# One gate group of the token-major projection moved behind the z groups, in a hybrid GatedDeltaNet and retention block

## The chip, the core and the metric

The kernel runs on one core of a Trainium2 chip. The core has five engines with an instruction queue each: TensorE (PE, matmuls, with its weight loads listed apart), VectorE (DVE), ScalarE (ACT), GpSimd (POOL) and SyncE (SP), which here only issues DMA transfers. Each engine runs its instructions in the order of the program made for it and waits on semaphores for the others. The metric is the device time of one execution in microseconds.

## The reference, cut to what matters

One layer of a diffusion backbone works on 1024 latent and 256 context tokens, D = 1024, all in float32. All projections come from one matrix, w_in; four heads of 128 are gated DeltaNet, four are retention.

```
p = (h @ w_in).astype(f32)                 # h: 256 context + 1024 latent tokens
qkv_a, z, ab, rq, rk, rv, rg = jnp.split(p, splits, axis=-1)
qkv_a = short_conv(...)                    # 5 taps, then silu
q, k, v = ...                              # q, k normalized
# gated delta rule, forward and backward, per chunk of 64:
A   = strict lower part of (beta k k^T) * decay
sol = triangular_solve(A + I, [beta v, beta k exp(G)])
# scan over the chunks with the solved rows
o_gdn = rms_norm(o_f + o_b) * silu(z)
o_ret = head_group_norm(r_f + r_b) * silu(rg)      # retention, rotary q and k
x = x + g1 * (concat(o_gdn, o_ret) @ w_out)
x = x + g2 * swiglu(...)
```

The columns `rg` (512 of them, the gate of the retention heads) are computed and passed through silu long before they are used: they multiply the retention's output at the end of the mixer. `z` is the same for the delta rule's output.

## The kernel before

Every float32 matmul is split into a high and a low half: `whi·hhi`, `wlo·hhi`, `whi·hlo`, three matmuls for one (lines 371 to 373 in `tm_half`, 611 to 613 in `conv_block`). ScalarE rounds the raw weights to `whi`, VectorE (or GpSimd) subtracts for `wlo` (L344, L345).

The projections whose result is wanted with tokens on partitions go by `token_major(g, ...)`. There are ten groups `g` of 256 columns, two for each of rv, rk, rq, rg and z, in this order of numbers: 6 and 7 are the retention's gate, 8 and 9 are z, 2 and 3 rk. A latent group has 8 tiles of 128 tokens and 24 matmuls a tile, 192 matmuls. The bank is called `tm`; gate and z groups leave it through `fin_gate`, a Silu on ScalarE (L532) into `res`, and a store to DRAM. The weights come from a pool with two buffers: `W`, which the convolutions use too, or `W2`, opened for the first groups and closed before the chunk preparation.

The stages around the change, in the order of the code:

1. `conv_block` for k, then q (blocks 4 to 7 and 0 to 3): matmuls into `b2`, two evictions on ScalarE (`u`, `y`: L614, L615), taps on VectorE (L621), Silu (L624).
2. `token_major` of the gate groups 6 and 7, then the pools `R2` and `W2` are closed, and the pools of the chunk preparation (`gu`, `gi`, `gp`) open over their space.
3. Chunk preparation, `pre(t)`, for ten chunks in three batches, `[0,1,2,9]`, `[3,8,4,7]`, `[5,6]`. PE multiplies `kk` (L705), transposes q (`qt`, L710) and multiplies `kq` (L715). For each of two directions SP loads a row of decays to all partitions (`gw`, L718), GpSimd masks it to `e` (L722), ScalarE takes the exp per head (L726) and then of `gw` itself (L735), VectorE multiplies `ut` (L730) and `sp` (L732), GpSimd the second half of `sp` (L736). All of `gw`, `e`, `ut`, `sp` have two buffers.
4. `invert(b)` after each batch: the 32 x 32 diagonal blocks of the triangular matrix are inverted by 31 serial steps, each a product (L765) and a subtraction (L767) on VectorE. Its inputs `L` come from a load `yr`, copied by ScalarE (L758) and VectorE (L759); `X` is cleared by GpSimd (L755).
5. The four v convolution blocks, their transposes `vT` (L856) and evictions `vt` (L859). `vT` and `tm` share three PSUM buffers.
6. `merge(b)`: small matmuls `m` (L807 to L834) join the inverted blocks, from `U` and `t`, loaded back from DRAM (`xd`, `un`).
7. `token_major` of z, groups 8 and 9, in pool `W`.
8. The scan: two directions, ten steps each, from loads `pk`; its first matmuls are `Tr` (L922). The remaining groups, rk among them, are computed beside it. Then come the retention, the output projection and the feed-forward part.

The order of each engine's instructions isn't that of the code. The program is made under a scheduler that simulates a timeline and lets each engine take what its simulation finds ready, so stages 3 to 8 run interleaved, and a change in one place moves rows in others. A buffer that is used again is waited for tile by tile.

Of the kernel before, what the change touches and what calls it, by code (L numbers as in the profile page):

```python
# [38 lines left out]
def build(nc, tc, ap, dbg=None, stop=None, marks=None):  # L39
    root = ExitStack()  # L40
    V, S, G, T, SY = nc.vector, nc.scalar, nc.gpsimd, nc.tensor, nc.sync

    def pool(name, bufs=1, side=None, space=None):
        kw = {}
        if side is not None:
            kw["side"] = side
        if space is not None:
            kw["space"] = space
        if space is not DRAM:
            kw["reuse_waits"] = "tile"  # L50
        es = ExitStack()
        p = es.enter_context(tc.tile_pool(name=name, bufs=bufs, **kw))
        root.push(es)
        p_close[id(p)] = es
        return p
# [10 lines left out]
    def checkpoint(name):  # L66
        if dbg is not None:
            marks.append((name, int(nc.cur_bb.bb.instructions[-1].name.split("-")[-1])))
        if stop == name:
            raise Stop()  # L70
# [120 lines left out]
    try:  # L191
# [40 lines left out]
        W2 = None  # L232
# [127 lines left out]
        def tm_weights(g, kh, pl, q=S):  # L360
            return weights(ap["wt"][g, :, 4 * kh:4 * kh + 4, :], [4, 256], V, pl, q, raws.get((g, kh)), g == 0)

        def tm_bank(g):
            return bank_a("tm")[:, 0:WIDE if g == 0 else 256]

        def tm_half(o, w, kh, t):

            tsl = slice(t * P, (t + 1) * P)
            whi, wlo = w
            for k in range(4 * kh, 4 * kh + 4):  # L370
                T.matmul(o, hhi[:, k, tsl], whi[:, k % 4, :], start=(k == 0), stop=False)  # L371
                T.matmul(o, hhi[:, k, tsl], wlo[:, k % 4, :], start=False, stop=False)  # L372
                T.matmul(o, hlo[:, k, tsl], whi[:, k % 4, :], start=False, stop=(k == KT - 1))  # L373
# [5 lines left out]
        def tm_store(g, t, o, finish, store, pl):  # L379
            early = g < 2  # L380
            res = (W2 if early else R1).tile([P, 256], F32, tag="res", name="res", bufs=4 if early else 2)
            finish(t, o[:, 0:256], res)
            if g == 0:
                S.activation(xa[:, t, :], o[:, 256:WIDE], AF.Copy)
            nm, c0 = GROUPS[g // 2], (g % 2) * 256
            dst = zd[t - 2, :, c0:c0 + 256] if nm == "z" else rd[t, :, RD[nm], c0:c0 + 256]
            store.dma_start(dst, res)

        def token_major(g, tiles, finish, store, pl, q=S):

            w = [tm_weights(g, kh, pl, q) for kh in range(2)]

            for p in range(0, len(tiles), 2):
                pair = [(t, tm_bank(g)) for t in tiles[p:p + 2]]
                for kh in range(2):
                    for t, o in pair:
                        tm_half(o, w[kh], kh, t)
                for t, o in pair:
                    tm_store(g, t, o, finish, store, pl)
# [47 lines left out]
        W2 = pool("w2", bufs=2)  # L447
# [86 lines left out]
        LAT, ALL = list(range(2, TT)), list(range(2, TT)) + [0, 1]  # L534
# [148 lines left out]
                        y[:, NCTX:].rearrange("p (t j) -> p t j", j=P))  # L683

        checkpoint("q")
        for g in (6, 7):
            token_major(g, LAT, fin_gate, S, W2, SY)
        checkpoint("rg")
        close(R2)
        close(W2)  # L690
# [185 lines left out]
        merge(2)  # L876


        for g in (8, 9):
            token_major(g, LAT, fin_gate, S, W)  # L880
        checkpoint("rgz")
        close(GM)
# [772 lines left out]
```

## Time and profile before

| | |
|---|---|
| median of 3 runs | 1476.76 us (1476.37 to 1479.9) |
| profiled execution | 1477.96 us, of which the trace's span 1476.2 us |
| granted TensorE clock, mean | 0.983 |
| PE busy | 1397.2 us, 95% of the span |
| VectorE busy | 964.6 us, 65% |
| ScalarE busy | 614.0 us, 42% |
| GpSimd busy | 590.3 us, 40% |

Times in the trace are microseconds from the start of the span. A row of a list of instructions has start, length, engine, line, operation, output and inputs, shape, and in brackets the idle time before it and what ended that. A row of waits has the engine and its line, what it waited for, then the total, the number of times and the longest. Group rows end in busy time, mean ns of one, and idle time before. Line numbers of the kernel before are used; in the changed kernel all lines behind the first edit are one lower.

The stages above lie here in the trace: the last gate group's matmuls 249 to 276, chunk preparation and v convolutions to 377, z and the merges to 473, the scan from 473, the retention from 580.

### The profile page before, as it was taken

How to read it: one execution, taken by the hardware profiler on the slowest of the kernel's cores; microseconds unless marked ns; L12 is line 12 of the kernel's file. 1: busy time of each engine (PE TensorE's matmuls, PEld its weight loads, DVE VectorE, ACT ScalarE, POOL GpSimd, SP SyncE). 2: the span in 40 equal slices, each digit the busy share in tenths (PEclk: the TensorE clock that was granted, in tenths of full speed). 3: DMA queues.
4: the chain of work that ended last, by engine and by line, in shares of the span. 5: the costliest groups of instructions: out<-in, count | busy, mean ns of one | idle time of the engine just before them, and what ended most of it. 6: DMA issues, size and time to landing. Idle time of an engine off the chain costs nothing.

```text
span 1476.2 us, 24111 instructions
## 1 busy us (share of the span) xinstructions
PE 1397.2 (95%) x8919; PEld 1199.2 (81%) x8919; DVE 964.6 (65%) x1856; ACT 614.0 (42%) x1326; POOL 590.3 (40%) x501
## 2 busy tenths in 40 slices
PE   7999999986789999899799899999999999999997
PEld 2898888975689999898688688877888888788885
DVE  6566789289792435689676877556555564657477
ACT  5643564587333111245443623233333332444445
POOL 0120010243202344234144688898555552335321
PEclk9999999998899999999899999999999999999999
DMA  9536686688888625996532265674222242776863
GB/s 337 197 105 205 189 249 200 219 264 277 282 216 277 238 76 178 416 341 209 184 125 104 97 238 210 242 264 162 105 97 105 107 151 79 260 260 194 288 216 114
DMA packets 170421, 298.14 MB, mean 202 GB/s; under 512 B 43496, under 2 KB 93880, under 8 KB 165952
## 3 DMA queue, kind: packets, MB, share of 16 engines
q1 hardware_dynamic: 118752, 253.17, 50.2%
q10 hardware_dynamic: 49072, 35.83, 7.8%
q0 software_dynamic: 2480, 7.60, 1.4%
q8 instruction: 70, 1.15, 0.3%
q14 instruction: 47, 0.39, 0.1%
HBM read 206.60 MB, written 89.96 MB: 201 GB/s over the span
## 4 chain that ended last, share of the span: by engine, by line
PE 55%; POOL 6%; DMA 5%; DVE 4%; issue 2%; ACT 2%; SPq 1%; ACTq 0%; POOLq 0%; DVEq 0%
PE ffn L1344 7%; PE ffn L1342 6%; PE ffn L1343 6%; PE fo L1470 4%; PE fo L1469 4%; PE fo L1468 4%; PE tm L371 3%; PE tm L373 3%; PE tm L372 3%; PE op L1203 2%; PE op L1201 2%; PE op L1202 2%; DMA wd<-tw 2%; POOL ws L1315 1%; DMA pk<-sd 1%
## 5 line engine op out<-in xcount | busy, mean ns | idle before, releaser
L371 PE MATMUL tm<-whi,hhi 128*128 128x256 f32 (+1 forms) x704 | 199.5, 287 | 7.7 <-ACT vt L859 3.4
L372 PE MATMUL tm<-wlo,hhi 128*128 128x256 f32 (+1 forms) x704 | 199.3, 285 | 2.4 <-issue 2.0
L373 PE MATMUL tm<-whi,hlo 128*128 128x256 f32 (+1 forms) x704 | 197.7, 285 | 0.0
L371 PEld LDWEIGHTS tm<-whi,hhi 128*128 128x128 f32 x704 | 132.8, 190 | 11.8 <-ACT vt L859 3.6
L1342 PE MATMUL ffn<-t,whi 128*128 128x512 f32 x352 | 136.9, 390 | 1.3 <-ACT whi L344 1.3
L1344 PE MATMUL ffn<-t,wlo 128*128 128x512 f32 x352 | 137.0, 390 | 1.0 <-DVE wlo L345 1.0
L1343 PE MATMUL ffn<-t,whi 128*128 128x512 f32 x352 | 137.0, 389 | 0.0
L372 PEld LDWEIGHTS tm<-wlo,hhi 128*128 128x128 f32 x704 | 133.7, 190 | 2.1 <-issue 0.9
L373 PEld LDWEIGHTS tm<-whi,hlo 128*128 128x128 f32 x704 | 132.8, 190 | 2.6 <-issue 1.8
L344 ACT ACTIVATE whi<-wraw 128x512 fp32r<-128x512 f32 (+2 forms) x98 | 75.1, 771 | 141.4 <-PE ffn L1343 80.5
L344 ACT ACTIVATE whi<-ws 128x512 fp32r<-128x512 f32 x88 | 55.6, 632 | 171.5 <-PE ffn L1343 123.4
L345 DVE TENSOR_TENSOR wlo<-ws,whi 128x512 fp32r<-128x512 f32 x88 | 93.9, 1068 | 47.0 <-ACT whi L344 46.8
L1469 PE MATMUL fo<-wlo,ahi 128*128 128x512 f32 x308 | 120.2, 390 | 2.1 <-DVE wlo L345 2.1
L1468 PE MATMUL fo<-whi,ahi 128*128 128x512 f32 x308 | 119.3, 390 | 0.7 <-ACT ahi L344 0.7
L1470 PE MATMUL fo<-whi,alo 128*128 128x512 f32 x308 | 119.0, 390 | 0.0
L345 DVE TENSOR_TENSOR wlo<-wraw,whi 128x512 fp32r<-128x512 f32 (+2 forms) x92 | 99.4, 1082 | 24.6 <-ACT whi L344 24.6
L1342 PE MATMUL ffn<-b,whi 128*128 128x512 f32 x264 | 103.8, 393 | 4.4 <-ACT whi L344 4.4
L1344 PE MATMUL ffn<-b,wlo 128*128 128x512 f32 x264 | 103.6, 393 | 0.8 <-DVE wlo L345 0.8
L1343 PE MATMUL ffn<-b,whi 128*128 128x512 f32 x264 | 103.4, 392 | 0.0
L612 PE MATMUL b<-hlo,whi 128*128 128x512 f32 (+1 forms) x256 | 94.4, 369 | 0.0
L613 PE MATMUL b<-hhi,wlo 128*128 128x512 f32 (+1 forms) x256 | 94.3, 368 | 0.0
L611 PE MATMUL b<-hhi,whi 128*128 128x512 f32 (+1 forms) x256 | 94.3, 368 | 0.0
(446 smaller groups left out, 3448.1 us busy)
## 6 DMA issues: line engine op xcount, KB each, us to landing
adaw<-ada SPq DMA_DIRECT2D x48, 512.0 KB, 4.4
pk<-sd SPq DMA_DIRECT2D x16, 1536.0 KB, 10.0
wraw<-wfi SPq DMA_DIRECT2D x44, 512.0 KB, 3.7
ar<-ad SPq DMA_DIRECT2D x33, 512.0 KB, 4.7
w<-wfo SPq DMA_DIRECT2D x22, 512.0 KB, 5.7
wd<-tw SPq DMA_DIRECT2D x11, 1024.0 KB, 4.8
ad<-act SPq DMA_DIRECT2D x20, 512.0 KB, 3.0
raw<-wd SPq DMA_DIRECT2D x20, 512.0 KB, 4.9
```

The source lines that it names most:

```text
L344: S.activation(hi, raw, AF.Copy)
L345: e.tensor_tensor(lo, raw, hi.bitcast(F32), ALU.subtract)
L371: T.matmul(o, hhi[:, k, tsl], whi[:, k % 4, :], start=(k == 0), stop=False)
L372: T.matmul(o, hhi[:, k, tsl], wlo[:, k % 4, :], start=False, stop=False)
L373: T.matmul(o, hlo[:, k, tsl], whi[:, k % 4, :], start=False, stop=(k == KT - 1))
L612: T.matmul(o, whi[:, k, :], hl, start=False, stop=False)
L1342: T.matmul(o, whi[:, k, :], xhi(xn, slice(0, 4), k), start=(first and k == 0), stop=False, **kw)
L1343: T.matmul(o, whi[:, k, :], xlo(xn, slice(0, 4), k), start=False, stop=False, **kw)
L1344: T.matmul(o, wlo[:, k, :], xhi(xn, slice(0, 4), k), start=False, stop=(k == 3), **kw)
L1468: T.matmul(po[g][i], ahi[:, ts], whi, start=(j == 0 and not kw), stop=False, **kw)
L1469: T.matmul(po[g][i], ahi[:, ts], wlo, start=False, stop=False, **kw)
L1470: T.matmul(po[g][i], alo[:, ts], whi, start=False, stop=(j == FH - 1), **kw)
```

## The change

Group 7, the second half of the retention's gate columns, is no longer computed with group 6 but after the z groups. Its call has the default pool `W` and ScalarE's queue for the weight load, where it had `W2` and SP's queue. So `R2` and `W2` are closed, and the pools of the chunk preparation opened, behind group 6.

```diff
         checkpoint("q")
-        for g in (6, 7):
-            token_major(g, LAT, fin_gate, S, W2, SY)
+        token_major(6, LAT, fin_gate, S, W2, SY)
         checkpoint("rg")
         close(R2)
         close(W2)
@@
-        for g in (8, 9):
+        for g in (8, 9, 7):
             token_major(g, LAT, fin_gate, S, W)
         checkpoint("rgz")
```

The scheduler makes new orders from this. Three places show it.

On PE, after the last matmuls of group 6 (bank `tm_2590`): before, the v convolution (`b2`) is broken off for the tiles of group 7, `tm_2657` to `tm_2826`, whose last rows and the first `kk` behind them are

```order
L372 MATMUL tm_2826<-wlo_2652,hhi_86 128x256
L373 MATMUL tm_2826<-whi_2651,hlo_87 128x256
L705 MATMUL kk_2897<-kc_2895 128x128 x4
L705 MATMUL kk_2930<-kc_2928 128x128 x4
L613 MATMUL b2_3572<-hhi_86,wlo_3539 128x512
```

and now the v convolution's matmuls run on without a tile of group 7, up to

```order
L612 MATMUL b2_3463<-hlo_87,whi_3429 128x512
L613 MATMUL b2_3463<-hhi_86,wlo_3430 128x512
L611 MATMUL b2_3463<-hhi_86,whi_3429 128x512
L704 MATMUL kk_2661<-kc_2659 128x128 x4
L612 MATMUL b2_3463<-hlo_87,whi_3429 128x512
```

The first `kk` stood behind all 192 matmuls of group 7 and 35 of the convolutions; it now stands behind 103 matmuls of the convolutions, in the second block.

On ScalarE, at the exps of the last chunk (`e_4137` and `e_4155` before, `e_3901` and `e_3919` now, one for each direction): before, the last convolution's Silu `y_3918` and all z tiles came behind them,

```order
L726 ACTIVATE e_4137<-e_4137,nG_1284 128x128 x3
L735 ACTIVATE gw_4135<-gw_4135 128x512
L712 ACTIVATE qt_4121,nq_1292<-qt_4121 128x128
L726 ACTIVATE e_4155<-e_4155,nG_1284 128x128 x4
L735 ACTIVATE gw_4153<-gw_4153 128x512
```

and now the Silu of z tiles (`res`, L532) stands between them, with loads of the activation table:

```order
L725 ACTIVATE e_3901<-e_3901,nG_1284 128x128 x4
L734 ACTIVATE gw_3899<-gw_3899 128x512
L532 ACT_TABLE_LOAD
L532 ACTIVATE res_4838<-tm_4788 128x256
L387 DMA zd_116<-res_4838 128x256
L532 ACTIVATE res_4841<-tm_4789 128x256
L387 DMA zd_116<-res_4841 128x256
L757 ACTIVATE L_3196<-yr_3191 64x1024
L725 ACT_TABLE_LOAD
L725 ACTIVATE e_3919<-e_3919,nG_1284 128x128 x4
```

The program has 24 table loads in all, where it had 20. On VectorE the product `ut` of `e_3919` now stands behind the third product of the second inversion; before, it came within the first.

On PE at the scan's first matmuls: before, tiles of the rk group (`tm_5542` to `tm_5674`) stood ahead of them,

```order
L372 MATMUL tm_5675<-wlo_5531,hhi_86 128x256
L373 MATMUL tm_5675<-whi_5530,hlo_87 128x256
L371 MATMUL tm_5674<-whi_5536,hhi_86 128x256
L372 MATMUL tm_5674<-wlo_5537,hhi_86 128x256
L834 MATMUL m2_4917<-U2_4813,xt2_4918 64x64 x16
L922 MATMUL Tr_5444<-pk0_5440 128x128 x4
```

and now the tiles of group 7 (`tm_5204` to `tm_5373`) do, and those of rk come behind:

```order
L371 MATMUL tm_5373<-whi_5198,hhi_86 128x256
L372 MATMUL tm_5373<-wlo_5199,hhi_86 128x256
L373 MATMUL tm_5373<-whi_5198,hlo_87 128x256
L921 MATMUL Tr_5444<-pk0_5440 128x128 x4
L921 MATMUL Tr_5451<-pk1_5442 128x128 x4
L371 MATMUL tm_5542<-whi_5530,hhi_86 128x256
```

Between the last `vT` and the first `Tr` stood 384 matmuls of z and 122 of rk; now 384 of z and 192 of group 7 stand there. Further back, one scan step more is complete ahead of the retention's first product.

## The prediction

> **What bounds the kernel now.** I read the windows by stage first, to find where TensorE (PE) is not busy, then the waits there, then the timeline around the longest ones. The stage table of the kernel before (window, its length in us, then busy us and instruction count of PE, PE weight loads, VectorE, ScalarE, GpSimd; granted clock, DMA share, GB/s):
>
> ```profile
> 249.00:276.30 27.30, 27.30 (x214) 25.74 (x213) 10.90 (x17) 9.15 (x20) 1.27 (x2) 1.00 0.49 147
> 276.30:355.00 78.70, 73.33 (x441) 62.97 (x439) 61.80 (x90) 64.46 (x177) 33.92 (x33) 1.00 0.85 270
> 355.00:377.10 22.10, 6.11 (x31) 5.66 (x31) 19.84 (x29) 16.00 (x50) 8.56 (x7) 0.64 0.78 246
> 377.10:400.00 22.90, 19.52 (x160) 19.31 (x159) 16.44 (x44) 4.96 (x14) 4.67 (x4) 0.97 0.94 314
> 400.00:441.90 41.90, 35.37 (x947) 33.44 (x946) 38.65 (x105) 12.16 (x22) 0.95 (x1) 0.96 0.87 209
> 441.90:473.50 31.60, 30.35 (x527) 28.62 (x525) 9.22 (x19) 10.87 (x21) 5.88 (x12) 1.00 0.83 254
> 473.50:580.50 107.00, 107.00 (x916) 106.85 (x915) 44.62 (x139) 12.11 (x16) 45.70 (x91) 1.00 0.46 172
> ```
>
> PE is full up to 276.3 and full again from 473.5 to 580.5. Between them it idles 5.4 + 16.0 + 3.4 + 6.5 + 1.2 = 32.5 us. So a gain in this part is only possible by taking from those 32.5 us: PE's work itself does not shrink. What holds PE there is a chain on other engines: the chunks' exps on ScalarE, then the inversions on VectorE (31 serial pairs of L765 and L767 in each of three batches, each step needing the one before), then the merges. The waits of PE between 276 and 474, the waits of all engines between 262 and 376, and the timeline show it:
>
> ```profile
> PE vT L856 <- ACT y L624: 9.6, 2, 9.3
> PE kk L705 <- issue: 8.4, 3, 6.7
> ...
> POOL e L722 <- DMA gw<-grow_d: 49.4, 12, 21.0
> DVE ut L730 <- POOL X L755: 15.7, 1, 15.7
> ...
> POOL X L755 <- PE tm L373: 7.1, 1, 7.1
> ```
> ```profile
> 388.22 1.06 ACT L758 ACTIVATE L<-yr 64x1024 f32<-64x1024 f32 x1 [0.42 <-DMA xd<-XT]
> 389.32 0.20 DVE L765 TENSOR_TENSOR tmp<-L,X 128x31 f32<-128x31 f32 x1 [5.03 <-ACT L L758]
> 441.89 1.12 DVE L769 COPY XT<-X 64x1024 f32<-64x1024 f32 x1
> 473.45 2.05 PE L922 MATMUL Tr<-pk 128*128 128x128 f32 x16
> ```
>
> VectorE is idle 15.7 us early, because the inversion's buffer X is cleared only after the gate's matmuls (group 7, ended at 276.3), and 5.0 us at 384 to 389 before the second inversion. The third inversion ends at 441.9. The scan's first matmul (Tr) comes 31.6 us later, and after it PE is work-bound for 107 us. So Tr's time, set against the work done by then, decides this change.
>
> **The change, part by part.** *Group 7 leaves the front.* Its size is the matmuls of the token-major bank (tm) in the same windows:
>
> ```profile
> 249.00:276.30 27.30, 23.41 (x192) 23.04 (x191) 0.00 (x0) 2.41 (x7) 1.00 0.49 147
> 441.90:473.50 31.60, 22.25 (x174) 20.63 (x172) 3.28 (x12) 1.15 (x3) 1.00 0.83 254
> ```
> ```profile
> 471.69 0.28 PE L371 MATMUL tm<-whi,hhi 128*128 128x256 f32 x1
> 471.81 0.28 PE L372 MATMUL tm<-wlo,hhi 128*128 128x256 f32 x1
> 471.93 0.28 PE L373 MATMUL tm<-whi,hlo 128*128 128x256 f32 x1
> ```
>
> 8 tiles of 24 matmuls, 192 in all, one starting every 0.119 us: 22.8 us of PE. They move from a stretch where PE is full to one that lies ahead of Tr. In the order before, 384 matmuls of z and 122 of the retention's rk group stand between the last vT and Tr. After, 384 of z and 192 of group 7 stand there and none of rk. So Tr would be reached with 122 matmuls less of the total done: 122 × 0.119 = 14.5 us. Break-even is Tr at 473.45 − 14.5 = 459.0. Anything later costs, anything earlier gains, microsecond for microsecond, since PE is full behind it.
>
> *The preparation's opening.* One expects it 22.8 us earlier. The trace says less:
>
> ```profile
> 261.10 0.68 DVE L505 TENSOR_TENSOR row<-row,gr 1x512 f32<-1x512 f32 x1 [1.84 <-PE gr L504]
> 261.80 0.25 SPq L506 DMA_DIRECT2D grow<-row  x1
> 262.15 0.33 SPq L664 DMA_DIRECT2D kc<-sd  x1
> 263.01 0.82 SPq L718 DMA_DIRECT2D gw<-grow_d  x2
> ```
>
> The first loads (kc, gw) already leave at 262 to 263, behind a store on SP's queue that waits for an adaLN row, not for group 7. What waited for group 7 is the first kk at 276.3 and the clearing of X. In the order after, kk stands 103 convolution matmuls behind the last tile of group 6; at the stretch's 73.33/441 = 0.166 us these take 17.1 us from 249, so the first kk comes near 267, some 9 us earlier. The exps show the pace from there:
>
> ```profile
> L726 ACT ACTIVATE e<-e,nG x80: 384/388/413, 268.5 to 371.2; 128x128 f32<-128x128 f32 x80
> ```
> ```profile
> gw<-grow_d SPq DMA_DIRECT2D x20, 256.0 KB, 4.8
> ...
> wraw<-wt ACTq DMA_DIRECT2D x4, 512.0 KB, 5.8
> ```
>
> Ten chunks of 8 exps take 268.5 to 371.6, 103.1 us. The pace is the buffer loop of gw (load 4.8, select, exps, gw's exp, sp, next load) together with ScalarE's other duties, and none of these gets shorter. I therefore keep no more than some 6 us of lead at the early chunks, and nothing at the last one: its exps end where they did, or 4 us later (below).
>
> *VectorE's chain to Tr.* This is the term that counts.
> - The 15.7 us of idle early: the taps (L621) of the first v convolution can stand there, since that convolution starts on PE 22.8 us earlier. From below: 0, if all is late. From above: 15.7. ScalarE must first evict the convolution's blocks, so part of the hole stays; I take two thirds, −10.
> - The 5.0 us before the second inversion: between 0 and −5.0. Its copy L waits on ScalarE behind a vt whose store was waiting; the order after puts that vt earlier. I take −5.
> - Group 7's two low halves of weights (wlo) now stand between steps of the third inversion:
>
> ```profile
> L345 DVE TENSOR_TENSOR wlo<-wraw,whi 128x1024 fp32r<-128x1024 f32 x4 | 4.9, 1215 | 0.0
> ```
>   2 × 1.2 = +2.4 us.
>
> From 441.9 to Tr (stores, loads, merge) I change nothing: 31.6 us. Sum: Tr at 473.45 − 10 − 5 + 2.4 = 460.9, against a break-even of 459.0: **+1.9 us**. With the bounds: 473.45 + 2.4 = 475.9, which is +16.9; 473.45 − 20.7 + 2.4 = 455.2, which is −3.8.
>
> *ScalarE.* z's Silu, and its table, now alternate with the exps of the last chunk: 24 table loads instead of 20.
>
> ```profile
> L726 ACT ACT_TABLE_LOAD x5 | 6.4, 1283 | 0.9 <-ACT res L532 0.8
> L624 ACT ACT_TABLE_LOAD x4 | 5.1, 1283 | 0.1
> ```
> ```profile
> 372.44 1.28 ACT L624 ACT_TABLE_LOAD   x1
> 373.73 1.27 ACT L624 ACTIVATE y<-y 128x1280 f32<-128x1280 f32 x1
> ```
>
> 4 × 1.283 = 5.1 us of ScalarE, of which some 4 before the last exps. The activation starts right behind the load, so 1.28 is the whole price here. ScalarE has 6.1 us idle in the 22.1 before 377.1, and the last chunk belongs to the third batch, whose inversion starts only after the second: I cost it at 0. Without that cover it is +5.1. [...]
>
> *Behind Tr.* The order finishes one more scan step before the retention's first product. That step's loads leave a stretch where DMA is full:
>
> ```profile
> 620.00:628.00 8.00, 6.23 (x50) 5.66 (x48) 4.60 (x16) 1.87 (x9) 2.08 (x2) 1.00 1.03 411
> 628.00:702.00 74.00, 69.17 (x608) 67.93 (x607) 64.77 (x242) 37.74 (x123) 30.87 (x28) 1.00 0.78 274
> ```
>
> 3 MB (two pk of 1536 KB) at 411 GB/s are 7.7 us that no longer compete at 620 to 628, where PE idles 1.8 of 8 us. Bounds: 0 and −7.7; nearest is the small idle, so −2. On the other side the denser scan could add waits; I add nothing.
>
> Sum: 1.9 + 0 − 2 = −0.1 on the profiled execution's 1477.96 (span 1476.2, 1.8 around it), which lies 1.2 above the median. The forecast is **1477 us, no change**.
>
> **The rivals.** *Faster: the pace of the chunks was PE's order, not the loop.* The mean pace is 103.1/10 = 10.3 us per chunk. The loop alone has these rows:
>
> ```profile
> L722 POOL TENSOR_SCALAR_AFFINE_SELECT e<-gw x20: 634/636/1707, 267.9 to 369.2; 128x512 f32<-128x512 f32 x20
> L736 POOL TENSOR_TENSOR sp<-gw,qc x16: 1264/1299/2011, 287.1 to 372.7; 128x512 f32<-128x512 f32 x16
> ```
> Load 4.8 + select 0.64 + four exps 1.3 + gw's exp 0.6 + sp 1.3 = 8.6 us. If PE's kk no longer stands behind conv matmuls, 8 intervals × 1.7 = 13.6 us come on top, the z tiles start near 360, and PE, with 32.5 us to take from, gets about 12 of them: 1465 us. For it: GpSimd waits 49.4 us for gw. Against: those waits are loads, and the loads wait for buffers that PE doesn't hold.
>
> *Slower: VectorE is stopped inside the second inversion.* In the order after, the last chunk's second product (ut) stands after the third step of the second inversion. Its exps stand on ScalarE behind two evictions of z tiles, so behind four z tiles on PE: 96 × 0.119 = 11.4 us after z starts, then a copy of 1.06, a table load 1.28 and exps 1.3. The second inversion would reach that point at about 375, so this decides as soon as z starts after 361. With z at 367 it holds VectorE 6 to 7 us, and with every microsecond of it Tr is later: 1477 + 8 = 1485 us. For it: in the order before, that product came in the first inversion, ahead of all z. Against: z needs only the last vT, and the convolutions that feed it start 22.8 us earlier.
>
> *Slower: the preparation does not open earlier.* The loads at 262 are as before, and if ScalarE's evictions hold the first taps too, only the 5.0 us are gained: Tr at 470.9, break-even missed by 11.9: 1489 us. That is the change not doing what it says.
>
> **How the numbers follow.** A measurement of this kernel can't tell changes within 0.3% (4.4 us) from none. The forecast, gain and loss balanced within that, has 0.36; the faster rival, with its weaker forms around 1470, has 0.34; VectorE stopped has 0.21; no earlier opening has 0.09. So faster 0.34, same 0.36, slower 0.30. The likeliest case's own range is 1473 to 1481, from Tr at 457 to 465. Eight in ten needs both sides: 1463 (the faster rival with 2 us more) to 1488 (the stopped VectorE, and most of the unopened case).
>
> **What would show it.** Right: first kk near 267, last exps at 368 to 376, first L765 of the second inversion at 374 to 380, third inversion's end at 427 to 431, Tr at 457 to 465, then PE full. The faster rival: exps of ten chunks in under 92 us, z's first tm before 355, Tr below 455. The stopped VectorE: a ut <- ACT e wait of over 4 us between steps of the second inversion. The unopened case: first kk after 274 or a VectorE idle of over 10 us still before 277. Wrong altogether: a change in the time of more than 5 us made before 249 or after 720, where I expect the order to do nothing.

## The result

The changed kernel takes 1486.93 us (median of 5 runs, 1484.14 to 1493.3), the kernel before 1477.23 us in the same comparison. The ratio is 1.0061, with a 95% interval of 1.0044 to 1.0078: slower by 0.61%, some 9 us. The forecast was no change, 1477 us; the result lies near the upper end of the range, on the side that had 0.30.

The profiled execution took 1488.32 us, its span is 1486.5 us, 10.3 longer than before. All of it is there when the scan begins. The stage table of the changed kernel, with the same columns as before; the cuts are its own first kk (266.3), last vT (354), the ends of the three inversions (370.8, then 402.8 as the third one's start, 434.5) and the first Tr (469.3):

```profile
249.00:266.30 17.30, 17.30 (x88) 13.76 (x87) 11.94 (x18) 6.44 (x11) 0.31 (x3) 1.00 0.41 105
266.30:354.00 87.70, 68.48 (x382) 59.05 (x381) 65.28 (x92) 71.04 (x196) 35.76 (x30) 0.87 0.81 268
354.00:370.80 16.80, 16.00 (x136) 15.60 (x135) 15.89 (x35) 14.23 (x41) 7.65 (x7) 0.99 1.03 307
370.80:402.80 32.00, 25.46 (x362) 24.30 (x360) 29.78 (x71) 10.71 (x18) 4.21 (x4) 0.95 0.98 281
402.80:434.50 31.70, 24.19 (x638) 22.90 (x639) 24.70 (x67) 9.87 (x18) 0.95 (x1) 0.89 0.71 206
434.50:469.30 34.80, 33.40 (x587) 31.54 (x587) 4.78 (x7) 12.44 (x25) 0.00 (x0) 0.95 0.78 260
469.30:580.50 111.20, 111.20 (x957) 111.20 (x956) 48.19 (x151) 15.08 (x22) 42.43 (x84) 1.00 0.53 187
```

TensorE (PE) is free of group 7 in front, has less to do there (68.5 of 87.7 us busy, at a granted clock of 0.87; before, the clock was 1.00 to 355.0 and 0.64 from there to 377.1) and is full without a stop only from Tr on. Where it stands still shows in its waits from 370 to 470:

```profile
PE m L813 <- issue: 5.7, 2, 2.9
PE m L816 <- issue: 4.6, 2, 3.4
PE tm L372 <- DVE wlo L345: 2.8, 1, 2.8
PE m L806 <- DMA t<-xd: 2.0, 3, 1.2
PE tm L371 <- ACT res L532: 0.4, 1, 0.4
```

The timelines of VectorE and PE show the chain that the prediction followed: the first inversion's end, the second's first step, the merge's negated copies (xt) and group 7's low halves (wlo) within the third inversion, its end, and Tr.

```profile
370.81 1.13 DVE L768 COPY XT<-X 128x1024 f32<-128x1024 f32 x1
373.19 0.21 DVE L764 TENSOR_TENSOR tmp<-L,X 128x31 f32<-128x31 f32 x1
400.65 1.05 DVE L768 COPY XT<-X 128x1024 f32<-128x1024 f32 x1
416.29 0.69 DVE L830 TENSOR_SCALAR xt<-m 128x512 f32<-128x512 f32 x1 [4.24 <-PE m L829]
421.57 0.69 DVE L830 TENSOR_SCALAR xt<-m 128x512 f32<-128x512 f32 x1 [0.23 <-PE m L829]
424.75 1.22 DVE L345 TENSOR_TENSOR wlo<-wraw,whi 128x1024 fp32r<-128x1024 f32 x1 [0.43 <-ACT whi L344]
434.55 1.04 DVE L768 COPY XT<-X 64x1024 f32<-64x1024 f32 x1
469.28 1.95 PE L921 MATMUL Tr<-pk 128*128 128x128 f32 x16
```

Against the kernel before: first inversion's end −10.2 us (370.8, it was 381.0), second's −14.6 (400.65, it was 415.24), third's only −7.3 (434.55, it was 441.89), Tr only −4.2 (469.28, it was 473.45). Over two thirds of the second inversion's lead is gone at Tr.

How little is left undone can be counted. Behind Tr stand 864 token-major matmuls, before it was 742, so 122 × 0.119 = 14.5 us of work came behind Tr while Tr came 4.2 us earlier: 10.3 us, which is the whole change of the span.

### The profile page after: what moved, and what is told of

Its sections match the earlier page's. It is cut to its first block, busy times and chain, and to the rows that moved or that the text cites. A ratio compares the mean times of both kernels' runs of the same rounds, so it can differ in the third digit from the quotient of the medians.

```text
span 1486.5 us, 24120 instructions
## 1 busy us (share of the span) xinstructions
PE 1401.4 (94%) x8919; PEld 1203.7 (81%) x8919; DVE 968.2 (65%) x1856; ACT 620.4 (42%) x1330; POOL 593.3 (40%) x501
## 3 DMA queue, kind: packets, MB, share of 16 engines
q8 instruction: 70, 1.15, 0.3%
## 4 chain that ended last, share of the span: by engine, by line
PE 51%; DMA 7%; DVE 6%; POOL 6%; issue 3%; ACT 2%; SPq 1%; ACTq 0%; POOLq 0%; DVEq 0%
PE ffn L1343 7%; PE ffn L1342 7%; PE ffn L1341 7%; PE tm L372 3%; PE tm L373 3%; PE tm L371 3%; PE fo L1468 3%; PE fo L1467 3%; PE fo L1469 3%; DMA wd<-tw 2%; PE op L1202 2%; PE op L1200 2%; PE op L1201 2%; DVE wlo L345 1%; POOL ws L1314 1%
## 5 line engine op out<-in xcount | busy, mean ns | idle before, releaser
L345 DVE TENSOR_TENSOR wlo<-ws,whi 128x512 fp32r<-128x512 f32 x88 | 90.9, 1034 | 41.0 <-ACT whi L344 40.7
```

The lines of the kernel that those rows point to most:

```text
L345: e.tensor_tensor(lo, raw, hi.bitcast(F32), ALU.subtract)
```

## The experiments

Every run is compared with the kernel before on the same chip. The table holds, from each one's profiled execution, the end of the last vT, the start of Tr, the granted clock between the two, the token-major matmuls left behind Tr, and what the break-even rule of the prediction gives, (Tr − 473.45) + 0.119 × (matmuls left − 742), beside the span's measured difference to 1476.2. The rule takes Tr as measured: it is an account of what lies behind Tr and does not say when Tr comes. The span is that of the one profiled execution, the ratio that of all, so the two differ by some microseconds: after_both's profile is of its slowest execution, g8_early's of its fastest.

| kernel | ratio to before (95%) | last vT | Tr | clock | left | rule | span |
|---|---|---|---|---|---|---|---|
| before | 1 | 377.4 | 473.4 | 0.98 | 742 | 0 | 0 |
| changed | 1.0061 (1.0044 to 1.0078) | 354.5 | 469.3 | 0.94 | 864 | +10.3 | +10.3 |
| no_g7 | 0.9995 (0.9980 to 1.0009) | 354.7 | 481.0 | 0.86 | 629 | −5.9 | +2.1 |
| g7_front_W | 1.0038 (1.0022 to 1.0054) | 378.5 | 479.3 | 0.91 | 740 | +5.6 | +4.7 |
| after_xtACT | 1.0106 (1.0089 to 1.0124) | 353.7 | 472.4 | 0.90 | 864 | +13.5 | +16.3 |
| after_both | 1.0083 (1.0065 to 1.0101) | 353.8 | 473.2 | 0.88 | 864 | +14.3 | +17.5 |
| after_s16 | 1.0113 (1.0087 to 1.0140) | 354.1 | 472.9 | 0.91 | 864 | +14.0 | +14.2 |
| after_s32 | 1.0090 (1.0072 to 1.0109) | 358.6 | 472.3 | 0.92 | 852 | +11.9 | +9.7 |
| before_s32 | 1.0066 (1.0046 to 1.0086) | 381.7 | 484.1 | 0.92 | 735 | +9.8 | +5.8 |
| g8_early | 0.9990 (0.9979 to 1.0001) | 395.6 | 491.5 | 0.93 | 575 | −1.9 | −5.3 |
| g8_early_wP | 1.0013 (0.9999 to 1.0026) | 395.2 | 496.1 | 0.92 | 588 | +4.3 | +3.0 |
| before_wP | 1.0089 (1.0063 to 1.0115) | 377.1 | 476.2 | 0.85 | 838 | +14.2 | +12.3 |
| after_wP | 1.0105 (1.0083 to 1.0127) | 351.0 | 477.8 | 0.89 | 850 | +17.2 | +18.7 |
| g7_twice | 1.0203 (1.0180 to 1.0225) | 400.4 | 503.3 | 0.93 | 734 | +28.9 | +28.2 |

**Without group 7 (no_g7).** From the changed kernel, group 7 is taken out: this kernel leaves the second half of the gate uncomputed and stores group 6's result in its place.

```diff
-        for g in (8, 9, 7):
+        for g in (8, 9):
             token_major(g, LAT, fin_gate, S, W)
...
             store.dma_start(dst, res)
+            if g == 6:
+                store.dma_start(rd[t, :, RD[nm], 256:512], res)
```

> Group 7 is not computed: group 6's result is stored in its place too, so the second half of the gate is wrong and 192 matmuls (22.8 us of TensorE) are missing. Theory V (the changed kernel's loss arises where VectorE's third inversion is stopped by the merge's products and carries group 7's two weight halves): the front lies ahead of a full TensorE, so the place in front cost about its work. By the order, 629 token-major matmuls stand behind the scan's first matmul instead of 742 before, 13.4 us less; with that matmul at 463 to 469 the time is 1453 to 1459 us. Theory P (TensorE simply has too much to do ahead of the scan in the changed kernel): the same here, since the 192 are gone; it differs by the other runs. A third reading (the place in front was mostly free cover, the chunk preparation being the limit anyway): 1465 us or more.

Measured: no difference to the kernel before, 0.9995. 22.8 us of PE's work are gone and nothing is won. Theory V's time fails, the third reading's comes. The windows from 276.3 (the first kk of the kernel before; here it comes at 265.4) to the last vT, from there to the second inversion's start, then to the third inversion's end, to Tr and behind it:

```profile
276.30:354.70 78.40, 57.42 (x331) 49.44 (x330) 57.34 (x84) 64.86 (x182) 29.82 (x27) 0.87 0.81 267
354.70:377.40 22.70, 21.63 (x163) 21.34 (x162) 17.78 (x36) 19.23 (x49) 7.98 (x7) 0.85 0.79 244
377.40:443.00 65.60, 53.63 (x969) 50.53 (x967) 52.88 (x142) 16.43 (x28) 7.42 (x11) 0.90 0.84 234
443.00:481.00 38.00, 36.17 (x631) 33.91 (x631) 9.97 (x25) 9.00 (x17) 8.58 (x18) 0.82 0.70 230
481.00:583.50 102.50, 101.19 (x866) 100.78 (x865) 42.26 (x137) 12.95 (x18) 38.38 (x80) 1.00 0.51 178
```

The last vT comes 22.7 us earlier, as much as was taken out. So the third reading's reason, that the chunk preparation is the limit anyway, does not hold: the whole 22.8 us have arrived at the last vT. They are lost behind it. PE idles 12.0 us from 377.4 to the third inversion's end and runs at 0.82 to 0.90 of its clock, and Tr comes at 481. Against the kernel before, PE's way from the last vT to Tr holds 3.7 us more of idle time, and its matmuls take 13.1 us longer than the count of them explains; another 8 us are lost behind Tr, where the rule gives −5.9 and the span is +2.1. The third inversion's end at 443.0 does not set Tr: the third merge's first matmul comes 23 us after it, without a wait.

**Group 7 in front, in the other pool (g7_front_W).** The pool and queue part of the change alone.

```diff
         GP = pool("gp")
+        token_major(7, LAT, fin_gate, S, W)
...
-        for g in (8, 9, 7):
+        for g in (8, 9):
```

> Group 7 stays in front, but in the convolutions' pool with its weights on ScalarE's queue, after the old pools are closed: the pool and queue part of the change alone. Theories V and P: no loss, 1474 to 1481 us, the first kk near 273 to 276, the scan's first matmul near 473. Rival W (the loss is the pool's: the convolutions' weights wait in the ring of two behind group 7's): about 1487 us, with TensorE idle before a convolution's matmuls for more than 5 us.

Measured: 1.0038, some 5.6 us slower, 0.6 of the changed kernel's loss. It is between the two expectations. The mechanism expected of rival W isn't in its waits: before a convolution's matmuls PE waits for nothing of note. Tr is 5.8 us later at nearly the same matmuls left, with a clock of 0.91 instead of 0.98 from the last vT on. Between the last vT and Tr the trace's record of the clock holds 17.5 us at half clock, where the kernel before has 4.4. The pools open early in this kernel too (X is cleared at 248.1), and that gains nothing either. A small move of rows costs over half as much as the change.

**The third inversion freed (after_xtACT, after_both).** In the first, the merge's negated copies go to ScalarE; in the second, group 7's low halves also go to GpSimd.

```diff
-            V.tensor_scalar(xt1.rearrange("p n j -> p (n j)")[:, :nu * 32], ps1[:, :nu * 32], -1.0, None, ALU.mult)
+            S.activation(xt1.rearrange("p n j -> p (n j)")[:, :nu * 32], ps1[:, :nu * 32], AF.Copy, scale=-1.0)
...
-                V.tensor_scalar(xt2.rearrange("p n j -> p (n j)"), ps1, -1.0, None, ALU.mult)
+                S.activation(xt2.rearrange("p n j -> p (n j)"), ps1, AF.Copy, scale=-1.0)
```

and, in after_both alone,

```diff
-            return weights(ap["wt"][g, :, 4 * kh:4 * kh + 4, :], [4, 256], V, pl, q, raws.get((g, kh)), g == 0)
+            return weights(ap["wt"][g, :, 4 * kh:4 * kh + 4, :], [4, 256], G if g == 7 else V, pl, q, raws.get((g, kh)), g == 0)
```

> The changed kernel, with the merges' negated copies (xt) on ScalarE instead of VectorE, so that the third inversion no longer waits for the merge's matmuls. Theory V: the third inversion ends 5 to 7 us earlier (427.5 to 429.5 instead of 434.5), the scan's first matmul near 463, 1479 to 1482 us. Theory P: the third inversion ends earlier, but the scan's first matmul stays within 2 us of 469, 1485 to 1489 us.

> As after_xtACT, and group 7's low weight halves are made by GpSimd instead of VectorE. Theory V: another 2.4 us, the third inversion ends near 426, the scan's first matmul near 461, 1476 to 1480 us. Theory P: no gain over the changed kernel, 1485 to 1489 us.

Measured: 1.0106 and 1.0083, neither faster than the changed kernel's 1.0061. Both theories miss: the times, 1494.5 and 1490.5 us, lie above the ranges of each. after_xtACT is no test of theory V, because its third inversion ends later, at 438.3: a low half of the weights waits 6.23 us for its high half from ScalarE, which now stands behind the copies that wait for the merge's matmuls. In after_both the third inversion holds nothing but its own steps; it starts at 406.9, 4.0 later than in the changed kernel, and ends at 431.8, 2.7 earlier. Still Tr comes at 473.2, 3.9 later than in the changed kernel. So in this run an earlier end of the third inversion does not bring Tr forward, against theory V. Its timeline and its windows up to the third inversion's end and from there to Tr:

```profile
431.81 1.09 DVE L768 COPY XT<-X 64x1024 f32<-64x1024 f32 x1
473.21 1.95 PE L921 MATMUL Tr<-pk 128*128 128x128 f32 x16
```
```profile
402.80:431.80 29.00, 23.65 (x526) 22.33 (x521) 26.48 (x71) 9.21 (x16) 3.41 (x2) 0.82 0.66 172
431.80:473.20 41.40, 35.68 (x732) 33.68 (x731) 2.31 (x2) 16.88 (x33) 2.34 (x1) 0.92 0.84 271
```

41.4 us now pass between the two where 31.6 did before. PE still has 732 instructions to run there, at a clock of 0.92 and with 5.7 us idle. From the last vT to Tr it needs 119.5 us for the 576 token-major matmuls that took 114.8 in the changed kernel, with 28.4 us at half clock instead of 13.7. That is nearer to theory P, by which PE's own way sets Tr, though the time goes into the clock and not into more work.

**The instruction loads shifted (after_s16, after_s32, before_s32).** Small matmuls of zeros at the very start, 16 as shown, 32 in the two others.

```diff
             T.matmul(psr[1][1], zero[:, 0:P], zero, start=True, stop=True)
+        for _ in range(16):
+            T.matmul(psr[1][1][:, 0:16], zero[:, 0:P], zero[:, 0:16], start=True, stop=True)
```

> The changed kernel with 16 small matmuls of zeros added at the very start, where TensorE waits for its first data; they only shift which of TensorE's instructions fall into one 16 KB instruction load. Theory F (the extra loss is TensorE standing still for its own instructions in the merges, and the half clock that follows): the stalls called issue between the last vT and the scan's first matmul (10.3 us in the changed kernel, 5.4 before) change by 2 us or more and the time moves with them, anywhere from 1478 to 1490 us. Theory D (the stalls come with the order, from full DMA queues): issue stalls within 1.5 us of 10.3, 1485 to 1490 us.

> The same with 32 small matmuls of zeros. Theory F: another pattern of stalls again, the scan's first matmul earlier or later than 469 by the change of the idle and half-clock sum, 1478 to 1490 us. Theory D: as the changed kernel, 1485 to 1490 us.

> The kernel before with the same 32 small matmuls of zeros. Theory F: the kernel before is as open to this as the changed one; its issue stalls rise from 5.4 or fall, 1474 to 1486 us. Theory D: as before, 1475 to 1480 us.

Measured: 1.0113, 1.0090 and 1.0066. Half of theory F holds. The stalls called issue between the last vT and Tr moved by about 2 us each time: 10.3 us in the changed kernel, 8.5 and 8.1 with the shifts; 5.4 before, 7.5 with the shift. So theory D, by which they would stay within 1.5 us of 10.3, falls. But the time did not follow the stalls: both shifted versions of the changed kernel have less of them, and neither is faster than it; after_s16 lies above both theories' ranges, and before_s32 just above theory F's. after_s16 and after_s32 have more half clock on that way, 21.0 and 17.1 us, where the changed kernel has 13.7. The edit was also less neutral than meant: the 32 matmuls delay PE's first real matmul from 7.5 to 15.9 us in before_s32, and 4.3 us of that are left at its last vT. Its clock from there to Tr is what stands out:

```profile
381.70:484.10 102.40, 91.54 (x1634) 87.44 (x1632) 64.17 (x166) 27.37 (x55) 11.48 (x17) 0.92 0.85 244
```

91.5 us of PE for 1634 instructions, where the kernel before needed 84.8 for 1627.

**z earlier, in the kernel before (g8_early, g8_early_wP).** The first z group ahead of the last v transposes; in the second, the low halves of groups 2, 8 and 9 by GpSimd.

```diff
             conv_block(8 + h, y, False)
+            if h == 3:
+                token_major(8, LAT, fin_gate, S, W)
...
-        for g in (8, 9):
-            token_major(g, LAT, fin_gate, S, W)
+        token_major(9, LAT, fin_gate, S, W)
```

> The kernel before (group 7 in front), with the first z group placed ahead of the last v transposes, so that its 192 matmuls can fill the 16 us in which TensorE idles at 355 to 377. By the order, 167 token-major matmuls more are done ahead of the scan's first matmul, 19.8 us. Reading by TensorE's idle: that matmul comes at 473 to 482, the clock stays at 1.00 around 360, 1458 to 1466 us. Reading by VectorE's chain (it now holds four products of the last chunk in the second inversion and four rope operations in the third): the third inversion ends after 450, the scan's first matmul after 488, 1472 us or more.

> g8_early with the low weight halves of the z groups and of the first rk group made by GpSimd (which is idle there) instead of VectorE. By the order 1524 token-major matmuls stand ahead of the scan's first matmul instead of 1370 before: 18.3 us. Reading by VectorE's chain: the four waits and pieces of 1.2 us leave the inversions, the third inversion ends 8 to 10 us earlier than g8_early's 452, the scan's first matmul comes at 480 to 484, 1465 to 1470 us. Reading by TensorE's account (needed time, idle, half of the half-clock time from the last vT on): that matmul stays near 490, 1474 to 1478 us.

Measured: 0.9990 and 1.0013, the same as before within 0.3%. In g8_early PE's hole at 355 to 377 is filled in part (15.7 of 22.1 us busy, where it was 6.1) and 167 matmuls more are done by Tr, but Tr comes 18 us later. By the numbers that is the reading by VectorE's chain (expected after 488, measured 491.5; the third inversion ends at 452.4). PE's rows tell another cause: the last vT already comes 18.2 us later, at 395.6, and the way from there to Tr takes 95.8 us, as long as before. The third merge's first matmul comes 24 us after the third inversion's end and waits for nothing. In g8_early_wP the third inversion ends 5.4 us earlier than that, at 447.0, and Tr still comes at 496.1, 4.6 later: again VectorE's gain doesn't reach Tr.

**z's and group 7's low halves on GpSimd (before_wP, after_wP).** One word in the weights' split, as above, for groups 8 and 9, and for 7, 8 and 9.

> The kernel before with z's low weight halves on GpSimd. VectorE loses 4.9 us from its inversions; the order puts 410 token-major matmuls between the last vT and the scan's first, not 506. Break-even reading: that matmul would have to come 11.4 us earlier, at 462, to hold the time; it comes 4 to 7 us earlier, so 1481 to 1485 us. Chain reading (only the end of the third inversion counts): 1470 to 1473 us.

> The changed kernel with the low weight halves of groups 7, 8 and 9 on GpSimd, the pair to before_wP. TensorE's account: the wait of 2.8 us for a low half goes, the scan's first matmul near 466 to 469 with 590 matmuls ahead of it, 1482 to 1486 us. Chain reading: the third inversion ends at 428 to 430, the scan's first matmul near 462, 1476 to 1480 us.

Measured: 1.0089 and 1.0105. Both are slower than their bases, and slower than either reading's range. The chain reading's premise doesn't come about: the third inversion ends at 448.8 and 441.5, later than in the bases, so these two runs don't test it. The other reading fails too: it had Tr between 466 and 470 in both, and it comes at 476.2 and 477.8. In before_wP the order puts 96 matmuls less ahead of Tr, yet Tr is 2.8 us later, not earlier: the first part of its way runs at a clock of 0.79, with 14.1 us idle.

```profile
377.10:448.80 71.70, 57.64 (x1039) 54.33 (x1040) 56.04 (x142) 21.74 (x43) 11.66 (x8) 0.79 0.83 229
448.80:476.20 27.40, 26.51 (x493) 24.81 (x492) 5.95 (x7) 8.89 (x19) 0.00 (x0) 1.00 0.77 240
```

The span is 12.3 us longer, the break-even rule gives 14.2 for that Tr.

**Group 7 twice (g7_twice).** The kernel before with one more pass of group 7.

```diff
-        for g in (6, 7):
+        for g in (6, 7, 7):
             token_major(g, LAT, fin_gate, S, W2, SY)
```

> The kernel before with group 7 computed twice in front, the same result stored a second time: 192 matmuls (22.8 us of TensorE) more. By the order these stand in the chunk preparation, between the first kk and the last vT, where TensorE idled 21 us. Reading by cover (leaving group 7 out of the front gained nothing, so this stretch is set by the other engines): the scan's first matmul stays within 473 to 482 and the time within 1477 to 1485 us. Reading by work (TensorE's matmuls count wherever they stand): 1495 to 1502 us.

Measured: 1.0203, some 30 us slower, more than the 22.8 us of work. The reading by cover fails, and the reading by work is passed. The last vT comes 23.0 us later, about the work that was added: PE idles 20.3 us between 276.3 and there, much as the 21.4 before, so the idle time took up next to nothing of it. PE's way from there to Tr takes 6.9 us more. The waits of all engines from 262 to 376 show what else moved:

```profile
POOL X L755 <- PE tm L373: 32.8, 1, 32.8
DVE ut L730 <- ACT e L726: 32.7, 5, 28.5
```

The inversion's X lies in space that the second pass still holds; it is cleared at 303.9 instead of 276.5, the first inversion starts at 349.2 instead of 314.2, and the rest follows. So a later opening of the pools goes along with a later chain; how much of the 23.0 us is its own and how much the 22.8 us of work, the run doesn't separate. Earlier is another matter: in the changed kernel X is cleared 29.5 us earlier (247.0) and the first inversion starts only 3.9 us earlier (310.3), because the exps of its fourth chunk come only 4.0 us earlier (288.9, they were at 292.9).

## Why the prediction was right or wrong

- *Break-even.* Right, and the part that carries furthest. "Tr earlier by 14.5 us or pay the rest" gives 10.3 us, measured are 10.3. Over the thirteen edited kernels the rule meets the span within 5 us in twelve; it fails by 8 in no_g7, where 113 matmuls fewer are left to fill the scan and the scan's own waits show (PE idles 16.8 of the 114 us from 606 to 720 there, 11.8 before).
- *The preparation's opening.* Right. First kk at 266.4 (forecast near 267); lead at the second chunk's exps 6.1 us, at the sixth 0.5; the last exps end at 374.2, 2.6 later than before (forecast 0 to 4). The rows of the exps:

```profile
L725 ACT ACTIVATE e<-e,nG x80: 384/388/410, 267.2 to 373.8; 128x128 f32<-128x128 f32 x80
L725 ACT ACT_TABLE_LOAD  x7: 1283/1283/1283, 265.7 to 371.7; - x7
```

- *VectorE's idle early, −10, and the 5.0 us ahead of the second inversion.* Both right: the first inversion ends 10.2 us earlier, the second starts without a wait and ends 14.6 us earlier (forecast 15).
- *Group 7's low halves, +2.4.* Right as such (2 × 1.22), but it was not all: the third inversion takes 31.6 us instead of 24.3, 7.3 more. The other 4.9 us are waits, 4.24 and 0.23 for the first merge's matmuls and 0.43 for a high half. I had the rival of VectorE being stopped inside an inversion, but put it in the second, by ut, where no wait arose; it happened in the third, by xt. None of the three rivals is what made the time: the chunks' exps take 107 us, not under 92, and the first kk comes at 266.4, not after 274.
- *"From 441.9 to Tr I change nothing: 31.6 us".* Wrong: 34.7. In that stretch PE is full (33.4 of 34.8 us), so the row that I took as VectorE's chain was already PE's.
- *The step that failed* is therefore the term "VectorE's chain to Tr": it was followed along the third inversion, as if a merge waited for that inversion and PE were ready whenever VectorE was. Tr was forecast at 460.9 and measured at 469.3, 8.4 us off. In neither kernel does PE wait for the third inversion. The first matmul of the third merge comes 15.5 us behind that inversion's end before and 17.2 in the changed kernel, and its row shows no wait. The last time that PE waits for anything but what the profile calls issue is a load of the first merge. The rows of that load and of the third merge, the kernel before first, then the changed one:

```profile
411.85 0.22 PE L814 MATMUL m<-U,xt 32*32 32x32 f32 x2 [0.93 <-DMA U<-xd]
457.38 0.75 PE L807 MATMUL m<-t,U 32*32 32x32 f32 x64
```
```profile
396.78 1.24 PE L806 MATMUL m<-t,U 32*32 32x32 f32 x122 [1.18 <-DMA t<-xd]
451.77 0.75 PE L806 MATMUL m<-t,U 32*32 32x32 f32 x64
```

  From there to Tr the chain is PE's own, and the lead of 15.1 us shrinks to 4.2. The waits of PE in that stretch of the kernel before, beside the 10.3 us of the changed kernel that stand in the result's list:

```profile
PE m L814 <- issue: 3.4, 2, 2.2
PE tm L372 <- issue: 2.0, 1, 2.0
```

  A sum along PE would have had Tr at 473.45 − 22.8 + 8.3 = 458.9, which is the break-even itself (the last vT earlier by the 192 matmuls, 70 more token-major matmuls behind it), so it wouldn't have forecast the loss either. What is missing in both sums is a term for PE's stops and clock on that way, and this is what was measured. From the last vT to Tr, PE takes 96.0 us before and 114.8 in the changed kernel, 18.8 more. 70 token-major matmuls more explain 8.3; idle rose from 11.2 to 16.2, 5.0, of which the waits called issue are 4.9 (5.4 before, 10.3 now); and the same kind of work took longer at a clock of 0.94 instead of 0.98, the remaining 5.5. The last two together are 10.5, beside the 10.3 us of the result. The trace's record of the clock supports the second: 13.7 us at half clock on this way, 4.4 before. In these stretches the token-major matmuls start every 0.213 us, beside them at the full clock every 0.119, so 9.3 us more of them are an estimated 4.1 us of lost work. The kernel before, then the changed one, each with all of PE's work and with its token-major matmuls alone:

```profile
377.40:473.40 96.00, 84.83 (x1627) 81.02 (x1625) 64.01 (x166) 27.69 (x55) 11.50 (x17) 0.98 0.87 248
377.40:473.40 96.00, 65.88 (x506) 62.61 (x505) 3.28 (x12) 6.13 (x16) 0.98 0.87 248
```
```profile
354.50:469.30 114.80, 98.59 (x1717) 94.28 (x1718) 74.65 (x179) 46.76 (x99) 12.81 (x12) 0.94 0.86 258
354.50:469.30 114.80, 77.70 (x576) 73.55 (x576) 0.00 (x0) 8.25 (x22) 0.94 0.86 258
```

  (The token-major matmuls take 77.7 us for 576, 0.135 each, where before it was 65.9 for 506, 0.130. These rows have no GpSimd column.)
- *Behind Tr, −2.* Not seen: the rule without it is right to 0.1 us. *ScalarE's table loads at 0:* nothing speaks against it; the exps have two more loads (7, it was 5), and their row ends 2.6 us later, ahead of a batch whose inversion starts some 29 us after.

What is shown, then: the 10.3 us appear between the last vT and Tr, as stops of PE and as matmuls at half clock, and the third inversion, on which the prediction had its term, is not what Tr waits for. Shortening it (after_both) did not bring Tr forward, and neither did giving PE fewer matmuls (before_wP). Leaving group 7 out gained nothing in the one order that was measured, though the last vT came 22.7 us earlier; computing it twice in front cost some 30 us. So the runs don't show that its place in front was free. What stays open is why an order stops PE more or less, and how much of the loss belongs to the move itself. Edits that are nearly neutral by their rows, g7_front_W and before_s32, cost 5.6 and 9.7 us (of the latter 4.3 may be its late start), and the kernel before has the highest granted clock (0.98) of all fourteen profiles in this stretch. A part of the change's 9 us may be the loss of that one order; no run separates it.

## What to carry to other kernels

Before moving work off a full engine, leave it out once. Here that gave no gain, which was a warning that the move had little to win; it does not show that the work is free where it stands, since the order of everything else changed as well. To price a move of filler work, take the first instruction behind which the engine is full and count what is done by then; time of that instruction plus work left behind it gave the end within 5 us for twelve orders out of thirteen. And before a term is worked out on one engine's chain, look whether the instruction that uses its result waits for it at all. Here it didn't, and the sum that counted was that of the other engine: its work, its stops and its clock.

## What the runs showed of the hardware

PE's stops called issue lie beside loads of instructions. The traces of both kernels record 70 loads of 16,384 bytes on a queue of the kind instruction (q8 on their pages: 70 packets, 1.15 MB), one for 255 of PE's 17,838 matmuls and weight loads. By that count and by the times below they are taken for PE's own. In the merges, where matmuls of 0.2 us overlap so that in the changed kernel 96 of them start in the microsecond from 405 us, just ahead of the second stall below, PE stops around such a load:

```profile
404.80 0.21 PE L816 MATMUL m<-xt,U 32*32 32x32 f32 x1 [3.35 <-issue]
409.07 0.26 PE L813 MATMUL m<-U,xt 32*32 32x32 f32 x2 [2.86 <-issue]
```

The loads ran from 402.50 to 403.45 and from 406.76 to 407.66 us, so PE went on 1.4 us after each had landed; the stall at 413.62 to 415.58 in the kernel before has its load at 413.26 to 414.22, and goes on 1.4 us after it. In the changed kernel's merges four such stalls take 10.3 us. Between the last vT and Tr the two kernels have seven waits called issue, three before and four in the changed kernel, and each of them ends 1.3 to 1.6 us after such a load has landed. That a load is what PE waits for is read from these times; no run takes the loads away.

The record of the granted clock in both kernels' traces holds 1.0 and 0.5 and nothing else. Its half-clock stretches last 3.41, 6.83, 10.24 and 23.89 us, all multiples of 3.41; only the one that runs past a trace's end has another length (7.50 and 7.81 us). In the changed kernel three such half-clock stretches lie between the last vT and Tr, and each begins 0.8 to 1.6 us after a stop of PE of 2.8 to 3.4 us; the one of 6.83 us, at 405.6 to 412.4, begins between the two stalls above. In the kernel before, one begins 0.4 us after the stall of 1.96 us, but none follows the stall of 2.19 us that ends at 440.98. The stretch of 3.41 us at 385.1 in the changed kernel is full of token-major matmuls, one every 0.213 us instead of 0.119: an estimated 1.5 us of lost work, beside the stop of 2.82 us ahead of it. That the stops bring the half clock about is not shown. In g8_early, with z's tiles in the hole at 355 to 377.1, the clock there was 0.85, where it was 0.64 before. And leaving 192 matmuls out (no_g7) took 7.6 us off PE's busy time up to 1475 us, not 22.8, while the mean granted clock went from 0.983 to 0.970.
